# Norms and output products of a hybrid diffusion step: 1/rms in PSUM, squares added one tile late, biases on ScalarE, other banks and held weights

## The chip, the cores and the metric

The kernel runs on one core of a Trainium2 chip. Times are microseconds on the device, from the first to the last work of one execution. Lower is better. The core has five engines that work side by side, each in its own order: TensorE (PE, the matmuls; PEld is its loading of weights), VectorE (DVE), ScalarE (ACT), GpSimd (POOL) and SyncE (SP, which issues most of the DMAs). Matmuls write to PSUM, which the kernel divides into banks of 512 float32 columns; everything else lies in SBUF.

## The reference

One step of a small diffusion backbone with two layers. Text is 128 prompt tokens and 512 sample tokens with 1024 features. Layer 0 has an SSD mixer and a differential-attention mixer side by side, layer 1 an RG-LRU mixer; each is followed by a gated ConvFFN of width 2816. Each of the four sub-layers has this frame:

```python
def rmsnorm(x, g):
    xf = x.astype(jnp.float32)
    y = xf * lax.rsqrt(jnp.mean(xf * xf, axis=-1, keepdims=True) + EPS)
    return (y * g.astype(jnp.float32)).astype(x.dtype)

def modulate(h, shift, scale):
    return h * (1.0 + scale) + shift
```

The sub-layer's input is `modulate(rmsnorm(x), shift, scale)`. Its last step is an output product (1024 or 2816 features to 1024), multiplied by a gate and added to `x`. Shift, scale and gate come from a map of the conditioning vector, one set for prompt and one for samples.

## The kernel before

**Layout.** The residual `X` is one SBUF tile of 128 partitions x 8 feature tiles (kt) x 644 columns: 128 prompt columns, a gap of 4, 512 sample columns. A matrix product takes each operand as a high part and a rest (`hhi`, `hlo` of the text; `whi`, `wlo` or, for held weights, `hi`, `lo` of the weights), and makes three matmuls for each 128x128 tile of weights (L471, L472, L473). ACT casts a raw weight tile to its high part (L112, for held ones L126) and POOL subtracts for the rest (L117, L129) in pieces of 256 columns: four for a weight of 8 kt, two for one of 4 kt.

**Order of the work.** The program is written out by hand as one order. `after(n, f)` puts a step `f` n ticks later, a tick being the matmuls of one kt; so the steps of a norm are strewn between matmuls. Each engine runs what it got in that order, and waits by semaphores.

**Weights.** Raw tiles come through a ring of 3; split ones have 3 slots too. A weight marked "held" goes to a pool of its own (`W.over`), which is open only during the output product, so that both column parts can use it.

**Output products (`out_parts`).** The columns are cut into two parts (`hf` 0: the prompt and some of the samples; 1: the rest). In layer 0 and at the LRU's output these are 388 and 256 columns, at FFN 0's last down-projection 260 and 384. For each part come 8 output tiles in pairs, with PSUM from `bank(n)` (two `g` banks, in layer 0) or `wide_banks(n)`. Then `evac` empties each: DVE adds the gated product to `X` (`add_part`, L317), ACT squares it (L537, `sqt`), DVE adds the square to `sq` (L538).

**Norm (`norm_part`).** When all 8 tiles of a part are there: PE sums the squares over the partitions (L555), DVE makes mean plus epsilon (L557), POOL takes the power -1/2 (L559, `rstd`), PE spreads 1/rms over the partitions (L566) and ACT copies it from PSUM to SBUF, over `sq` (L570). Then `gen(kt)` for each kt: DVE multiplies 1/rms, scale and `X` (L317, `full` or `sqt` from `sq`), ACT adds the shift (L601). For an even kt the sum goes to `hhi` at once and DVE makes `hlo` with the shift (two L317). For an odd kt ACT adds it in place, casts to `hhi` (L604), and POOL makes `hlo` (L69). `low(kt-1)`, the making of `hlo`, stands behind the products of kt. Part 0's norm runs while PE does part 1 of the output product; PE may begin the next stage only after its last step (`k.fresh[0]`).

**The FFN's first products** use sums and differences of the normed tiles (`sums`, L1499 to L1503), which need the shift in `full` for all kt: for the even ones L1499 adds it. `part` makes `t24h` and `t24l` of one of them. The weights are summed likewise (`wsum`), and their parts are `shi` and `slo`.

**Map steps.** The map of the conditioning vector is done in small steps (`M.step`, `mt<-mraw`) between other products; `small()` gives them a PSUM bank, "m" or "o", which the norm uses too.

## Time and profile before

| | |
|---|---|
| median of 3 runs | 2109.64 us (2108.07 to 2111.09) |
| the profiled execution | 2112.0 us |
| its span in the trace | 2109.2 us |
| mean granted clock of TensorE | 0.956 of full speed |
| busy: PE | 1890.8 us (90%) |
| busy: DVE | 1431.1 us (68%) |
| busy: ACT | 963.7 us (46%) |
| busy: POOL | 1188.8 us (56%) |

The span reaches from the first to the last instruction; the execution's own time is 2.8 us longer. The busy share says how much of the span an engine worked. [...]

### The profile page before, as it was taken

To read this page: it belongs to the slowest core of one execution; us is meant where nothing else is said; L and a number is where in the kernel's file an instruction comes from. 1 tells how busy PE (TensorE), PEld (TensorE's weight loads), DVE (VectorE), ACT (ScalarE), POOL (GpSimd) and SP (SyncE) were. 2 spreads that over 40 slices of the span, in tenths; PEclk is the share of its full clock that TensorE was granted. 3 is DMA by queue.
4 is the path that set the end of the run, shared out by engine and by line. 5 is a ranking of instruction groups with operands and counts; after the bars stand their busy time and mean duration, and the time that the engine had idled before them with its cause. 6 is when DMAs were issued, how large, how long until landed. Compare 5 with 4: busy or idle time off the path is not lost. (4 is left out here: it accounts for less than half of the span.)

```text
span 2109.2 us, 33582 instructions
## 1 busy us (share of the span) xinstructions
PE 1890.8 (90%) x12601; PEld 1728.1 (82%) x12601; DVE 1431.1 (68%) x2454; ACT 963.7 (46%) x1670; POOL 1188.8 (56%) x1536
## 2 busy tenths in 40 slices
PE   6878889999999988999999997988778899999997
PEld 4767768888888877898889997877678799999986
DVE  3477756656664346687778787667857777877874
ACT  3454444455454334343344445577734444444444
POOL 3235454233344544477657785578855577776772
PEclk9889999999999998999999999999989899999998
DMA  9555432121113432435642222211111122222221
GB/s 257 171 164 164 151 108 66 49 55 48 38 49 122 127 123 71 125 121 163 187 141 63 72 87 75 60 46 46 40 50 41 44 76 81 85 87 70 62 78 63
DMA packets 255577, 196.59 MB, mean 93 GB/s; under 512 B 13837, under 2 KB 233816, under 8 KB 255288
## 3 DMA queue, kind: packets, MB, share of 16 engines
q1 hardware_dynamic: 252664, 184.59, 29.1%
q0 software_dynamic: 2528, 7.13, 1.4%
q8 instruction: 99, 1.62, 0.3%
q10 hardware_dynamic: 224, 2.73, 0.3%
q14 instruction: 62, 0.51, 0.1%
HBM read 187.50 MB, written 6.92 MB: 92 GB/s over the span
## 5 line engine op out<-in xcount | busy, mean ns | idle before, releaser
L117 POOL TENSOR_TENSOR wlo<-wraw,whi 128x256 fp32r<-128x256 f32 (+1 forms) x845 | 714.7, 874 | 554.7 <-ACT whi L112 488.2
L471 PE MATMUL wide<-hhi,whi 128*128 128x322 f32 (+4 forms) x1072 | 360.2, 336 | 49.9 <-DVE X L317 22.9
L472 PE MATMUL wide<-hlo,whi 128*128 128x322 f32 (+4 forms) x1072 | 346.1, 323 | 7.7 <-DVE hlo L512 7.5
L473 PE MATMUL wide<-hhi,wlo 128*128 128x322 f32 (+4 forms) x1072 | 342.7, 320 | 0.0
L112 ACT CAST whi<-wraw 128x1024 fp32r<-128x1024 f32 (+2 forms) x263 | 220.1, 838 | 146.3 <-PE wide L473 73.9
L471 PEld LDWEIGHTS wide<-hhi,whi 128*128 128x128 f32 x1072 | 213.1, 199 | 69.0 <-issue 23.0
L471 PE MATMUL gh<-hhi,whi 128*128 128x322 f32 (+3 forms) x704 | 236.5, 336 | 9.3 <-ACT zt L1161 8.7
L472 PEld LDWEIGHTS wide<-hlo,whi 128*128 128x128 f32 x1072 | 212.3, 198 | 13.0 <-DVE hlo L512 9.0
L472 PE MATMUL gh<-hlo,whi 128*128 128x322 f32 (+3 forms) x704 | 220.9, 314 | 1.3 <-DVE hlo L512 1.0
L473 PE MATMUL gh<-hhi,wlo 128*128 128x322 f32 (+3 forms) x704 | 220.2, 313 | 0.0
L473 PEld LDWEIGHTS wide<-hhi,wlo 128*128 128x128 f32 x1072 | 212.7, 198 | 0.0
L471 PE MATMUL wide<-hidh,whi 128*128 128x322 f32 (+4 forms) x624 | 200.5, 321 | 2.2 <-DVE ft L1585 2.2
L472 PE MATMUL wide<-hidl,whi 128*128 128x322 f32 (+4 forms) x624 | 196.0, 314 | 1.6 <-DVE hidl L512 1.6
L473 PE MATMUL wide<-hidh,wlo 128*128 128x322 f32 (+4 forms) x624 | 196.0, 314 | 0.0
L317 DVE SCALAR_TENSOR_TENSOR ft<-ft,PC 128x643 f32<-128x643 f32 x160 | 168.1, 1072 | 37.5 <-ACT ft L1527 35.5
L471 PEld LDWEIGHTS gh<-hhi,whi 128*128 128x128 f32 (+1 forms) x704 | 133.9, 190 | 34.8 <-issue 21.3
L1527 ACT ACTIVATE ft<-ft,PC 128x644 f32<-128x644 f32 x80 | 74.0, 927 | 144.6 <-DVE ft L1592 133.7
L317 DVE SCALAR_TENSOR_TENSOR X<-wide,modc,X 128x128 f32<-128x128 f32 (+3 forms) x264 | 123.5, 511 | 22.7 <-PE wide L473 22.7
L472 PEld LDWEIGHTS gh<-hlo,whi 128*128 128x128 f32 (+1 forms) x704 | 133.6, 190 | 2.4 <-DVE hlo L512 1.2
L473 PEld LDWEIGHTS gh<-hhi,wlo 128*128 128x128 f32 (+1 forms) x704 | 133.3, 189 | 0.6
L471 PEld LDWEIGHTS wide<-hidh,whi 128*128 128x128 f32 x624 | 119.4, 191 | 15.9 <-issue 7.0
L112 ACT CAST shi<-wsum 128x512 fp32r<-128x512 f32 x120 | 72.7, 617 | 122.2 <-DVE wsum L141 110.8
(381 smaller groups left out, 4579.5 us busy)
## 6 DMA issues: line engine op xcount, KB each, us to landing
wraw<-in_ffn_w_up_dram SPq DMA_DIRECT2D x88, 512.0 KB
mraw<-in_w_mod_dram SPq DMA_DIRECT2D x80, 512.0 KB
wraw<-in_ssd_attn_w_in_dram SPq DMA_DIRECT2D x42, 512.0 KB
wraw<-in_ffn_w_down_dram SPq DMA_DIRECT2D x96, 192.0 KB
E<-ad SPq DMA_DIRECT2D x16, 640.0 KB
mraw<-in_w_mod_dram SPq DMA_DIRECT2D x32, 256.0 KB
wraw<-in_ssd_attn_w_out_dram SPq DMA_DIRECT2D x16, 512.0 KB
wraw<-in_lru_w_in_dram SPq DMA_DIRECT2D x16, 512.0 KB
```

Of the source, the lines that this page charges most:

```text
L112: self.nc.scalar.copy(hi, src)
L117: low.tensor_sub(lo[:, q], src[:, q], hi[:, q].bitcast(F32))
L317: nc.vector.scalar_tensor_tensor(out, in0, scalar, in1, op0=op0, op1=op1, **kw)
L471: nc.tensor.matmul(ps[:whi.shape[-1], p0:p0 + c1 - c0], whi, xhi[:, c0:c1], start=start, stop=False)
L472: nc.tensor.matmul(ps[:whi.shape[-1], p0:p0 + c1 - c0], whi, xlo[:, c0:c1], start=False, stop=False)
L473: nc.tensor.matmul(ps[:whi.shape[-1], p0:p0 + c1 - c0], wlo, xhi[:, c0:c1], start=False, stop=stop)
L1527: after(at, lambda: nc.scalar.activation(out, u, AF.Identity, scale=par(cw, 2 * NF + t), bias=par(cb, t)))
```

## The change

1. `rstd_rows` leaves 1/rms in PSUM (bank "o"); the norm's products read it there, and ACT's copies L570 go, but for the one place where attention's norm uses it.
2. While that bank is in use, map steps take bank "m" alone (`k.spread`).
3. The square of an output tile is added to `sq` when the next tile has been emptied (`add_square`), the last one when the sum is needed.
4. In norms whose tiles are kept for the FFN (`keep`), ACT adds the shift of even kt in place and casts, as for odd kt; DVE makes `hlo` of a whole part with one subtraction. The additions L1499 in `sums` go, and L1501 moves from POOL to DVE.
5. In layer 0's output product two pairs of output tiles in three take a wide PSUM tile.
6. Instead of 3 everywhere, the number of output weights that are not held is 2 in layer 0, none at FFN 0's last down-projection, and 3 in the other two. And the look-ahead for weights no longer stops at the output product's last weight (`base + 7`).

```diff
-N_STD = 3
+N_STD = (2, 0, 3, 3)
...
         if n == 0:
+            add_square()
             nc.scalar.activation(sq, X[:, n, c0:c1], AF.Square)
         else:
             t = k.tmp.tile([128, NT], F32, name="sqt", tag=k.sq_tag, bufs=k.n_sqt)[:, c0:c1]
             nc.scalar.activation(t, X[:, n, c0:c1], AF.Square)
+            add_square()
+            k.square = sq, t
+
+    k.square = None
+
+    def add_square():
+
+        if k.square:
+            (sq, t), k.square = k.square, None
             nc.vector.tensor_add(sq, sq, t)
...
     def small():
-        return mtile("m" if k.narrow else None)
+        return mtile("m" if k.narrow or k.spread else None)
...
-    def rstd_rows(r, hf):
-
-        m = mtile()
+    def rstd_rows(r, hf, tag):
+
+        m = mtile(tag)
         for i in range(len(k.cut.chunks[hf])):
             nc.tensor.matmul(m[:, 128 * i:128 * i + 128], r[:, i:i + 1].to_broadcast([128, 128]), ident,
                              start=True, stop=True)
-        at = 0
-        for _, c0, c1 in k.cut.segs[hf]:
-            nc.scalar.copy(k.sq[:, c0:c1], m[:, at:at + c1 - c0])
-            at += c1 - c0
+        return m
...
-            if kt % 2:
+            if kt % 2 or keep:
                 c = slice(*k.cut.parts[hf])
-                pieces(nc.gpsimd, "tensor_sub", lo[:, c], t[:, c], h[:, c].bitcast(F32))
+                if kt % 2:
+                    pieces(nc.gpsimd, "tensor_sub", lo[:, c], t[:, c], h[:, c].bitcast(F32))
+                else:
+                    nc.vector.tensor_sub(lo[:, c], t[:, c], h[:, c].bitcast(F32))
                 return
...
-                    fma(t[:, c0:c1], k.sq[:, c0:c1], A, X[:, kt, c0:c1], op0=OP.mult, op1=OP.mult)
-                    nc.scalar.activation((t if kt % 2 else hhi[kt])[:, c0:c1], t[:, c0:c1], AF.Identity, bias=B)
-                if kt % 2:
+                    fma(t[:, c0:c1], box.m[:, at:at + c1 - c0], A, X[:, kt, c0:c1], op0=OP.mult, op1=OP.mult)
+                    nc.scalar.activation((t if whole else hhi[kt])[:, c0:c1], t[:, c0:c1], AF.Identity, bias=B)
+                    at += c1 - c0
+                if whole:
                     c = slice(*k.cut.parts[hf])
                     nc.scalar.copy(hhi[kt][:, c], t[:, c])
...
-                            W.upto(min(base + i + AHEAD, base + 7))
+                            W.upto(base + i + AHEAD)
...
+        turn = []
+
         def bank(n):
+
+            if n == 2:
+                turn.append(0)
+            if n == 2 and len(turn) % 3:
+                return wide_banks(2)
             return [k.psum.tile([128, 512], F32, name="gh", tag="g", bufs=2) for _ in range(n)]
...
                 x, y = full[kt], full[kt + 4]
-                if kt % 2 == 0:
-                    for i, t in ((kt, x), (kt + 4, y)):
-                        for s, cols in STREAMS:
-                            nc.vector.tensor_scalar(t[:, cols], t[:, cols], modc[l][:, s, 24 + i:25 + i], None, op0=OP.add)
                 nc.vector.tensor_sub(x[:, L], x[:, R], x[:, L])
-                nc.gpsimd.tensor_sub(x[:, R], y[:, R], x[:, R])
+                nc.vector.tensor_sub(x[:, R], y[:, R], x[:, R])
                 nc.vector.tensor_sub(y[:, R], y[:, R], x[:, L])
```

What this does to the order of the instructions is seen at three places. In the rows that follow, L317 is the helper for a multiply and add, and the lines of the changed kernel are some ten higher than those of before.

DVE, in part 1 of layer 0's output product, just ahead of the emptying of the third pair of output tiles (the first `X<-` in each). Before:

```order
L597 MEMSET full 128x4
L317 SCALAR_TENSOR_TENSOR full<-sq,acol_115,X 128x128
L317 SCALAR_TENSOR_TENSOR full<-sq,acol_115,X 128x256
L317 SCALAR_TENSOR_TENSOR hlo_88<-full,modc_112,hhi_80 128x128
L317 SCALAR_TENSOR_TENSOR hlo_88<-full,modc_112,hhi_80 128x256
L317 SCALAR_TENSOR_TENSOR X<-gh,modc_112,X 128x256
L538 TENSOR_TENSOR sq<-sq,sqt 128x256
```

The same place after the change:

```order
L607 MEMSET full 128x4
L317 SCALAR_TENSOR_TENSOR full<-mt,acol_115,X 128x128
L317 SCALAR_TENSOR_TENSOR full<-mt,acol_115,X 128x256
L597 TENSOR_TENSOR hlo_88<-full,hhi_80 128x388
L317 SCALAR_TENSOR_TENSOR X<-wide,modc_112,X 128x256
L548 TENSOR_TENSOR sq<-sq,sqt 128x256
```

The products read 1/rms from `mt` (PSUM), `hlo` is one operation, and the third pair stands in a wide tile; the norm's steps are still ahead of the emptying. The fourth pair takes `gh`, as the first did.

ACT, at the start of FFN 0's last down-projection, where the last hidden tile (`hidh`, the second of the two in the rows of before) is still being made: L1527 (L1550 after) are its convolutions, L1543 (L1566) its gate. Before:

```order
L112 CAST whi<-wraw 128x512
L508 CAST hidh<-ft 128x644
L112 CAST whi<-wraw 128x512
L1527 ACTIVATE ft<-ft,PC 128x644
L126 CAST hi_12883<-wraw 128x512
L1527 ACTIVATE ft<-ft,PC 128x644
L126 CAST hi_12902<-wraw 128x512
L126 CAST hi_12921<-wraw 128x512
L1543 ACTIVATE ft<-ft 128x644
L126 CAST hi_12939<-wraw 128x512
L508 CAST hidh<-ft 128x644
L126 CAST hi_12960<-wraw 128x512
```

After:

```order
L508 CAST hidh<-ft 128x644
L1550 ACTIVATE ft<-ft,PC 128x644
L126 CAST hi_12851<-wraw 128x512
L126 CAST hi_12858<-wraw 128x512
L126 CAST hi_12865<-wraw 128x512
L126 CAST hi_12872<-wraw 128x512
L1550 ACTIVATE ft<-ft,PC 128x644
L126 CAST hi_12891<-wraw 128x512
L126 CAST hi_12910<-wraw 128x512
L1566 ACTIVATE ft<-ft 128x644
L126 CAST hi_12928<-wraw 128x512
L508 CAST hidh<-ft 128x644
```

The casts `whi` of this product's first weights are gone; four held casts stand between the two convolutions, where one stood.

POOL, from the rests of the held weights of that product (`lo`) to the norm of part 0 behind it (`rstd` and the rests of odd kt, `hlo`); `wlo` are weights of the next stage. Before:

```order
L129 TENSOR_TENSOR lo_12940<-wraw,hi_12939 128x256 x2
L129 TENSOR_TENSOR lo_12961<-wraw,hi_12960 128x256 x2
L559 TENSOR_TENSOR rstd<-msq,expo 128x2
L69 TENSOR_TENSOR hlo_83<-sqt,hhi_75 128x130 x2
L69 TENSOR_TENSOR hlo_85<-sqt,hhi_77 128x130 x2
L117 TENSOR_TENSOR wlo<-wraw,whi 128x256 x12
L69 TENSOR_TENSOR hlo_87<-sqt,hhi_79 128x130 x2
```

After:

```order
L129 TENSOR_TENSOR lo_12929<-wraw,hi_12928 128x256 x2
L129 TENSOR_TENSOR lo_12950<-wraw,hi_12949 128x256 x2
L117 TENSOR_TENSOR wlo<-wraw,whi 128x256 x12
L570 TENSOR_TENSOR rstd<-msq,expo 128x2
L69 TENSOR_TENSOR hlo_83<-sqt,hhi_75 128x130 x2
L69 TENSOR_TENSOR hlo_85<-sqt,hhi_77 128x130 x2
L69 TENSOR_TENSOR hlo_87<-sqt,hhi_79 128x130 x2
```

The twelve `wlo` have moved from between the `hlo` to ahead of `rstd`; and eight `lo` of two pieces each stand ahead of them, where there were five.

## Rows read from the trace of the kernel before

**Rows 1.** Page, part 1: busy us, share of the span, instructions of each engine.

```profile
PE 1890.8 (90%) x12601; PEld 1728.1 (82%) x12601; DVE 1431.1 (68%) x2454; ACT 963.7 (46%) x1670; POOL 1188.8 (56%) x1536
```

**Rows 2.** Waits of PE, 730 to 800: who ended them, total us, times, longest.

```profile
PE gh L471 <- DVE X L317: 9.2, 5, 5.6
```

**Rows 3.** Timeline of PE: start, us, instruction, and the idle time before it.

```profile
744.37 0.42 PE L471 MATMUL gh<-hhi,hi 128*128 128x388 f32 x1 [1.29 <-DVE X L317]
```

**Rows 4.** Timeline of DVE, 760 to 800 us.

```profile
775.34 0.48 DVE L317 SCALAR_TENSOR_TENSOR full<-sq,acol,X 128x256 f32<-128x256 f32 x1
...
783.36 0.81 DVE L317 SCALAR_TENSOR_TENSOR full<-sq,acol,X 128x128 f32<-128x128 f32 x1
...
784.09 0.95 DVE L317 SCALAR_TENSOR_TENSOR full<-sq,acol,X 128x256 f32<-128x256 f32 x1
784.97 1.71 DVE L317 SCALAR_TENSOR_TENSOR hlo<-full,modc,hhi 128x128 fp32r<-128x128 f32 x2
...
791.38 0.47 DVE L317 SCALAR_TENSOR_TENSOR X<-gh,modc,X 128x256 f32<-128x256 f32 x1
```

**Rows 5.** Windows: busy time of each engine, granted clock (PEclk), DMA share, GB/s.

```profile
789.40:796.20 6.80, 4.30 (x20) 4.30 (x21) 3.70 (x7) 1.89 (x5) 4.38 (x7) 0.50 0.52 153
1315.00:1328.60 13.60, 7.84 (x36) 7.87 (x37) 5.42 (x11) 2.98 (x6) 7.02 (x13) 0.50 0.35 96
1598.40:1605.10 6.70, 5.06 (x17) 5.09 (x18) 1.11 (x4) 0.42 (x1) 0.70 (x1) 0.50 0.01 1
```

**Rows 6.** Waits of PE, 833 to 863 us.

```profile
PE wide L471 <- ACT shi L112: 3.8, 1, 3.8
```

**Rows 7.** Timeline of DVE, 825 to 837 us, in the sums.

```profile
825.83 1.26 DVE L1499 TENSOR_SCALAR full<-full,modc 128x128 f32<-128x128 f32 x4
...
828.50 1.01 DVE L1502 TENSOR_TENSOR full<-full 128x322 f32<-128x322 f32 x1 [0.99 <-POOL full L1501]
...
836.60 0.49 DVE L1502 TENSOR_TENSOR full<-full 128x322 f32<-128x322 f32 x1 [1.04 <-POOL full L1501]
```

**Rows 8.** Timeline of PE, first matmul of the LRU's input product.

```profile
1320.76 0.56 PE L471 MATMUL wide<-hhi,whi 128*128 128x260 f32 x1 [7.90 <-DVE X L317]
```

**Rows 9.** Timeline of ACT, 1271 to 1330 us.

```profile
1274.11 0.93 ACT L1527 ACTIVATE ft<-ft,PC 128x644 f32<-128x644 f32 x1 [2.53 <-DVE ft L1592]
```

**Rows 10.** Timeline of POOL, 1271 to 1330 us.

```profile
1275.66 10.41 POOL L129 TENSOR_TENSOR lo<-wraw,hi 128x256 fp32r<-128x256 f32 x10
1297.29 0.70 POOL L559 TENSOR_TENSOR rstd<-msq,expo 128x2 f32<-128x2 f32 x1 [11.22 <-DVE msq L557]
...
1308.43 9.26 POOL L117 TENSOR_TENSOR wlo<-wraw,whi 128x256 fp32r<-128x256 f32 x12 [2.89 <-issue]
1317.64 2.02 POOL L69 TENSOR_TENSOR hlo<-sqt,hhi 128x130 fp32r<-128x130 f32 x4
```

**Rows 11.** Timeline of DVE, 1271 to 1330 us.

```profile
1287.18 0.43 DVE L538 TENSOR_TENSOR sq<-sq,sqt 128x260 f32<-128x260 f32 x1 [0.48 <-ACT sqt L537]
...
1300.53 0.88 DVE L317 SCALAR_TENSOR_TENSOR sqt<-sq,acol,X 128x128 f32<-128x128 f32 x3
...
1310.21 2.32 DVE L317 SCALAR_TENSOR_TENSOR sqt<-sq,acol,X 128x128 f32<-128x128 f32 x3
...
1314.65 0.60 DVE L317 SCALAR_TENSOR_TENSOR X<-wide,modc,X 128x384 f32<-128x384 f32 x1
```

**Rows 12.** Waits of PE, 1593 to 1662 us.

```profile
PE wide L471 <- DVE lt L1856: 6.8, 1, 6.8
```

**Rows 13.** Timeline of DVE, 1593 to 1604 us.

```profile
1596.55 0.43 DVE L538 TENSOR_TENSOR sq<-sq,sqt 128x256 f32<-128x256 f32 x1 [0.48 <-ACT sqt L537]
```

**Rows 14.** Timeline of ACT, 784 to 800 us: bias on 128 and 256 columns, cast.

```profile
784.20 0.40 ACT L601 ACTIVATE full<-full,modc 128x128 f32<-128x128 f32 x1 [0.36 <-DVE full L317]
785.08 0.51 ACT L601 ACTIVATE full<-full,modc 128x256 f32<-128x256 f32 x1 [0.48 <-DVE full L317]
785.62 0.52 ACT L604 CAST hhi<-full 128x388 fp32r<-128x388 f32 x1
```

More of the change, by code (lines that the diff above doesn't have):

```diff
@@ L364, in add_w, with held @@
         items.append((ap[r0:r0 + 128 * kt, c0:c0 + w], kt, w, kind))
-    def held(n, n_std=3):
+    def held(n, n_std):
         return "held" if n >= n_std else None
@@ L394, in tile_hybrid_step @@
         for n in range(8):
-            add_w(w_out, 1024 * half, 8, 128 * n, kind=held(n, N_STD) if half else None)
+            add_w(w_out, 1024 * half, 8, 128 * n, kind=held(n, N_STD[0]) if half else None)
     def early(c):
@@ L414, in downs @@
             for n in range(8):
-                add_w(dn, 128 * starts[c], FF_CHUNKS[c], 128 * n, kind=held(n, N_STD) if last else None)
+                add_w(dn, 128 * starts[c], FF_CHUNKS[c], 128 * n, kind=held(n, N_STD[1 + 2 * l]) if last else None)
         for c, n in enumerate(FF_CHUNKS):
@@ L430, in tile_hybrid_step @@
     for n in range(8):
-        add_w(lw_out, 0, 8, 128 * n, kind=held(n))
+        add_w(lw_out, 0, 8, 128 * n, kind=held(n, N_STD[2]))
     ffn_items(1)
@@ L546, in small @@
     def small():
-        return mtile("m" if k.narrow else None)
+        return mtile("m" if k.narrow or k.spread else None)
     def rstd_cols(chunks):
-        m = mtile()
+        add_square()
+        m = mtile("m")
         n = len(chunks)
@@ L597, in gen @@
                     nc.vector.memset(t[:, NP:S0], 0.0)
+                whole, at = kt % 2 or keep, 0
                 for s, c0, c1 in segs:
                     A, B = acol[l][which][:, s, kt:kt + 1], modc[l][:, s, 24 * which + kt:24 * which + kt + 1]
[L600 to L602 removed]
+                    fma(t[:, c0:c1], box.m[:, at:at + c1 - c0], A, X[:, kt, c0:c1], op0=OP.mult, op1=OP.mult)
+                    nc.scalar.activation((t if whole else hhi[kt])[:, c0:c1], t[:, c0:c1], AF.Identity, bias=B)
+                    at += c1 - c0
+                if whole:
                     c = slice(*k.cut.parts[hf])
@@ L607, in gen @@
             k.fresh[hf] = kt == KD
+            k.spread = k.spread and kt < KD
             if kt == KD and then:
@@ L611, in norm_part, with rows @@
         after(at[0], cols)
-        after(at[0] + at[1], lambda: rstd_rows(box.r, hf))
+        def rows():
+            k.spread = True
+            box.m = rstd_rows(box.r, hf, "o")
+        after(at[0] + at[1], rows)
         for kt in range(KD + 1):
             after(at[0] + at[1] + at[2] + at[3] * kt, lambda kt=kt: gen(kt))
-    k.fresh = [True, True]
+    k.fresh, k.spread = [True, True], False
     k.cut = Cut(CUTS[0])
@@ L643, in gemm_parts, with out_parts @@
                     W.ahead()
-    def out_parts(xs, evac, then, banks, first, ready, n_std=N_STD):
+    def out_parts(xs, evac, then, banks, first, ready, n_std):
         ws, base = [], W.next
@@ L671, in out_parts @@
                     if j == len(late) - 1:
-                        W.upto(min(base + batch[-1][-1] + AHEAD, base + 7))
+                        W.upto(base + batch[-1][-1] + AHEAD)
                         break
@@ L1372, in rows @@
                 for hf in range(2):
-                    rstd_rows(rs[hf], hf)
+                    m, at = rstd_rows(rs[hf], hf, "m"), 0
+                    for _, c0, c1 in k.cut.segs[hf]:
+                        nc.scalar.copy(k.sq[:, c0:c1], m[:, at:at + c1 - c0])
+                        at += c1 - c0
                 for t in range(KD):
@@ L1440, in attention @@
         hctx = ExitStack()
-        out_parts(H, evac, then, bank, [[0], [1]], [ready])
+        out_parts(H, evac, then, bank, [[0], [1]], [ready], N_STD[0])
         W.over = None
@@ L1636, in then @@
                         until(lambda: k.fresh[0])
-                out_parts(xs, evac, then, wide_banks, [[0, 1], [2, 3], [4, 5]], [ready])
+                out_parts(xs, evac, then, wide_banks, [[0, 1], [2, 3], [4, 5]], [ready], N_STD[1 + 2 * l])
                 W.over = None
@@ L1849, in then @@
                     until(lambda: k.fresh[0])
-            out_parts(H, evac, then, wide_banks, [[0, 1], [2]], [lambda: until(lambda: len(k.scanned) == 8 and k.n_given == 14), ready], 3)
+            out_parts(H, evac, then, wide_banks, [[0, 1], [2]], [lambda: until(lambda: len(k.scanned) == 8 and k.n_given == 14), ready], N_STD[2])
             W.over = None
```

1 line of the change is left out of this document (removed).

## The prediction

> **What bounds the kernel now.** I read the page first: TensorE (PE) is busy 1890.8 us, nine tenths of the span [rows 1]. So work on another engine is worth only the PE idle time that it ends, plus what PE loses because its clock falls behind such a pause. Then I asked for PE's waits in the four stretches in which an output product ends, a norm is made and the next stage begins: 730 to 800 us (layer 0's output product) [rows 2], 833 to 863 us (the sums of FFN 0's first products) [rows 6], 1271 to 1330 us (FFN 0's last down-projection and the norm of layer 1) [rows 8], and 1593 to 1662 us (the LRU's output product and FFN 1's sums) [rows 12]. In three of the four, what ends the largest wait is DVE with an `X` (L317), an accumulator waiting to be emptied, or something that stands right behind such ones. Last I read the timelines of DVE, ACT and POOL in those stretches, to see what stands ahead of that instruction, and windows for the clock.
>
> **Stage A, layer 0's output product and FFN 0.** Two causes are added up in [rows 2]: 9.2 us in 5 waits.
>
> *More banks.* Before, each pair of output tiles takes both `g` banks, so the next pair starts only after DVE has emptied one. In column part 0 that costs PE 1.29 us [rows 3], twice in this form; with a smaller one it is 3.0 us. With two pairs in three in the wide banks, the next pair has a bank that was emptied long ago. I take 2.9; the bounds are 0 (if the wide bank is emptied as late) and 3.0.
>
> In column part 1 the longest wait, 5.6 us [rows 2], has another head: DVE came to the evacuation only at 791.38 us [rows 4], because the order shown above puts tiles of the norm ahead of it. The last pair now goes to the `g` banks, which pair 0 left long before; what stands ahead of the evacuation on DVE no longer holds PE. The 5.6 us go, and about 0.6 of small ones. [...] Sum for this place 8.3. It is worth this only if the norm of part 0 is also finished by then, since PE may not go on to FFN 0 before: that takes DVE's norm steps being shorter.
>
> *1/rms read from PSUM.* The trace has no DVE operation with 1/rms in PSUM. Nearest rows: `X<-gh` has one operand in PSUM and takes 0.47 us for 256 columns while POOL runs; `full<-sq`, both in SBUF, takes 0.95 for 256 while POOL runs and 0.48 alone [rows 4]. The bounds for the new form are thus 0.47 and 0.95; I take 0.47, since its operands are of the kinds of `X<-gh`. Four tiles of 0.81 + 0.95 [rows 4] then become 0.34 + 0.47 (by the same ratio), 3.8 us less on DVE. The two `hlo` of an even tile (1.71 together [rows 4]) become one subtraction. That one has two SBUF inputs; its bounds are 0.49 and 1.01, from the 322-column rows [rows 7], and I take 0.9. So DVE has about 5 us less ahead of the last norm step, and the norm ends in time.
> [...]
>
> *ACT's added work.* An even tile now has two biases and a cast, 0.40 + 0.51 + 0.52 = 1.43 us for 388 columns [rows 14], as an odd tile has already. For eight tiles that is 11.4 us against 9.4. Cover: part 1 of the output product, 192 matmuls of 256 columns. The copies L570 leave ACT. In part 1's own norm, which nothing covers, ACT's work per tile is about as long as DVE's was; I count it at nothing, bounds -1 and +1.
>
> *Sums.* Two of the four sums lose four L1499 (1.26 us), and each loses a wait of 1.0 us for POOL, for which a DVE operation of 0.49 comes [rows 7]. What stands behind the last of them is `t24h`, then the cast `shi`, for which PE waited 3.8 us [rows 6]. Not all eight L1499 and four waits lie on that chain, since DVE does other work between the sums; what moves `shi` is one 1.26 and two times 0.5, 2.3. I take 2.4, bounds 1 and 4. Behind it POOL's `slo` may be late next.
>
> Stage A: -2.9 - 8.3 - 2.4 = **-13.6** (bounds -5 and -17).
>
> **Stage B, FFN 0's last down-projection, the norm, the LRU.** Here a part of the change costs time. All eight weights are now held, and a held weight's cast is issued only within this output product. Before, PE began with weights cast earlier. Now all four first casts stand behind the convolution of 1274.11 us on ACT [rows 9], and the fourth, whose raw tile has no place until POOL has done the first, stands ahead of the gate's convolution. I estimate that `hid[21]` is ready 4 us later, and hence the first evacuation too.
> What comes back: in each tile's cycle of evacuation, ACT square and DVE add, DVE waits 0.48 us for the square [rows 11]. With the add one tile late that goes; eight tiles give 3.8 us. So the sum of squares is ready about when it was.
> Then POOL: `rstd` came at 1297.29, after ten `lo` pieces of 1.04 us from 1275.66 on [rows 10]. Sixteen end at about 1292, and the twelve `wlo` (9.26 us [rows 10]), which came after `rstd`, now come ahead of it: about 1302. That is 5 us later. But before, the `wlo` ran against the norm: three `sqt<-sq` took 2.32 us against 0.88 elsewhere [rows 11], and POOL's last `hlo` ended only at 1319.66 [rows 10]. In the same stretch the evacuation from PSUM still took 0.60 us [rows 11]. Now eight tiles at about 1 us of ACT each end near 1312, PE's part 1, which ended at 1312.9 before (1320.76 less the wait, [rows 8]), near 1315, the last evacuation near 1317. PE went on at 1320.76, after 7.9 us of waiting [rows 8]; I take 1318, -2.7. The lower clock behind that wait lasted 13.6 us, with PE busy 7.84 of it [rows 5], a loss of 3.9; a third of it back, -1.3. Stage B: **-4** (bounds -8 and +8; the upper one if `rstd` comes as late as 1311).
> [...]
>
> **Stage C, the LRU's output product and FFN 1.** PE waited 6.8 us for `lt` [rows 12], which stands behind four evacuations on DVE, each with a wait of 0.48 us for its square [rows 13]: 1.9 us less. Ahead of them stand norm steps as in stage A, some 3 us shorter. I take -4.8 (bounds -2 and -6). Of 6.7 us at 0.50 with PE busy 5.06 [rows 5], 2.5 come back. The sums are those of FFN 0: -2.4. Stage C: **-9.7** (bounds -4 and -12).
>
> The rest: map steps have almost none in these stretches, so leaving bank "o" alone costs nothing; if some did come, one would wait for the DVE add of the one before. The last FFN's evacuations save little, since PE waits there for another step. 0.
>
> **Sum.** -13.6 - 4 - 9.7 = -27.3. The profiled execution took 2112.0 us, so 2084.7; it lies 2.4 us above the median of the runs, 2109.64, from which the same sum gives 2082.3. I forecast 2083 (own range 2074 to 2093).
>
> **Rivals.**
> *The norm, not the bank, is late (0.17).* PE gets its banks, runs to the end of the product and waits there for the norm of part 0, whose pace ACT now sets. For: ACT has 2 us more in that norm, plus casts. Against: 5 us less on DVE, which was the slower. Half of 8.3 and of 4.8 + 2.5 would be lost: about 2091; with the sums' gain gone into `slo` too, 2096.
> *Reads from PSUM are dear (0.04).* If the new form takes the upper bound, 0.95 in place of 0.47, DVE's norm steps stay as long as beside POOL, and the 3.8 us that were to make each norm end in time are missing in stages A and C: 2091. Against: 0.47 and 0.60 for `X` [rows 4, 11]. [...]
> *The held weights turn stage B into a loss (0.12).* `rstd` waits on POOL behind `wlo`, which waits for raw tiles that can be fetched only when the last `lo` are done. Stage B at +8 in place of -4: 2095. It decides from a `rstd` later than about 1306 us.
> *Slower (0.10).* DVE works in order, and the subtraction of an even tile now waits for two biases and a cast on ACT, where it waited for one bias at a time. If that wait is not covered, a tile goes in series: 0.82 + 1.43 + 0.9 and hops, 3.3 us against about 2 in [rows 4], 9 us more a norm, with the evacuations behind it on DVE. Stages A and C would lose their gain at the banks and at `lt` and 9 us each besides, stage B its 4: about 2120. It decides when ACT needs over 2 us for a tile with its square and the weights' casts between. Against it: the subtraction stands behind the next tile's products on DVE, so a tile's time is there to cover it.
>
> **Chances.** Forecast 0.57, the rivals 0.17 + 0.04 + 0.12 + 0.10. The first three rivals end below 2100, the last above. About 0.2% (4 us) is what a measurement of this kernel can tell. Faster by more than that 0.82, within it 0.07 (the tails of the rivals), slower 0.11. The range takes the forecast's lower end, a little widened, 2072, and reaches to 2102 over the milder rivals.
>
> **What would show it.** In the profile after: no wait of PE for `X` of over 1 us in the output product of layer 0, and no stretch at half clock at its end; `full<-mt` at 0.34 and 0.47 us also beside POOL; DVE's waits for `sqt` gone; in stage B a later first evacuation, a later `rstd`, and a wait of PE before the LRU of about 5 us; in stage C a wait of about 2 us for `lt`. I am wrong if PE waits for the norm at the end of these products as long as it waited for the banks, or if stage B loses more than 8 us.

## The result and the profile after

The changed kernel takes 2080.66 us (median of 4 runs, 2078.34 to 2080.81), the kernel before beside it 2110.27; the ratio is 0.9857, with a 95% interval of 0.9844 to 0.987. Measured once more (`after_again`) it came to 0.9854 (0.9837 to 0.9871). The forecast was 2083, 2072 to 2102.

The page of the changed kernel, part 1, answers to [rows 1]:

```profile
PE 1880.9 (90%) x12601; PEld 1719.6 (83%) x12601; DVE 1415.1 (68%) x2438; ACT 964.7 (46%) x1677; POOL 1184.0 (57%) x1528
```

The matmuls are the same; PE's 10 us less of busy time go with a mean granted clock of 0.962 for 0.956 (the clock that TensorE was granted, 1 being its full speed). The rest of the gain lies in the waits. PE's waits in layer 0's output product, 720 to 800 us, against [rows 2]:

```profile
PE mt L332 <- DMA mraw<-in_w_mod_dram: 2.7, 1, 2.7
...
PE wide L471 <- DVE X L317: 0.7, 1, 0.7
```

Of the 9.2 us for `X` in the product nothing is left; the 0.7 belongs to the start of FFN 0 and stood in the kernel before too, at 800.43 us. But a wait stands there that the kernel before did not have: 2.7 us for the weights of a map step (`mraw`), in part 0. DVE's timeline in part 1 of the same product, against [rows 4]:

```profile
782.60 0.56 DVE L597 TENSOR_TENSOR hlo<-full,hhi 128x388 fp32r<-128x388 f32 x1 [2.54 <-ACT hhi L616]
...
783.35 0.47 DVE L317 SCALAR_TENSOR_TENSOR full<-mt,acol,X 128x256 f32<-128x256 f32 x1
783.74 0.47 DVE L317 SCALAR_TENSOR_TENSOR X<-wide,modc,X 128x256 f32<-128x256 f32 x1
...
789.91 0.48 DVE L317 SCALAR_TENSOR_TENSOR X<-wide,modc,X 128x256 f32<-128x256 f32 x1
```

`full<-mt` takes 0.47 us with POOL at work, and DVE reaches the third pair of output tiles, which stands behind norm steps, at 789.91 us (791.38 before). The first row shows the new wait of the change: `hlo` stands 2.54 us for ACT's cast, between weight casts. PE has no wait for `X` in this product, so it is covered. Over the whole program (groups by line and form: count, busy us, mean ns), before and then after:

```profile
L317 DVE SCALAR_TENSOR_TENSOR full<-sq,acol,X 128x256 f32<-128x256 f32 x32 | 19.1, 618 | 5.8 <-ACT sq L570 5.8
```

```profile
L317 DVE SCALAR_TENSOR_TENSOR full<-mt,acol,X 128x256 f32<-128x256 f32 x32 | 14.5, 474 | 3.9 <-PE mt L577 3.9
```

FFN 0's last down-projection and the LRU's start: PE's waits of 1255 to 1315 us, then ACT, DVE and POOL there, against [rows 8 to 11]:

```profile
PE wide L471 <- ACT hi L126: 3.9, 1, 3.9
...
PE wide L471 <- DVE X L317: 0.8, 1, 0.8
```

```profile
1266.62 1.64 ACT L126 CAST hi<-wraw 128x512 fp32r<-128x512 f32 x3
1271.71 0.62 ACT L126 CAST hi<-wraw 128x512 fp32r<-128x512 f32 x1 [3.44 <-DMA wraw<-in_ffn_w_down_dram]
```

```profile
1284.83 0.44 DVE L548 TENSOR_TENSOR sq<-sq,sqt 128x260 f32<-128x260 f32 x1
1285.19 0.59 DVE L317 SCALAR_TENSOR_TENSOR X<-wide,modc,X 128x128 f32<-128x128 f32 x2
```

```profile
1288.16 5.91 POOL L117 TENSOR_TENSOR wlo<-wraw,whi 128x256 fp32r<-128x256 f32 x8 [1.40 <-ACT whi L112]
1294.02 0.70 POOL L570 TENSOR_TENSOR rstd<-msq,expo 128x2 f32<-128x2 f32 x1
```

PE now waits 3.9 us at the front for the held casts; the fourth cast waits 3.44 us for its raw tile, with the second convolution behind it. DVE's square adds hardly wait any more. `rstd` stands behind the `wlo`. At the end the wait before the LRU is 0.8 us in place of 7.9. In the LRU's output product, 1570 to 1640 us, against [rows 12]:

```profile
PE wide L471 <- ACT shi L112: 4.2, 1, 4.2
...
PE wide L471 <- DVE lt L1879: 1.4, 1, 1.4
```

And the granted clock behind these three places (windows; the third figure from the right is PEclk), against [rows 5]:

```profile
788.40:795.00 6.60, 5.93 (x50) 5.76 (x49) 4.30 (x11) 3.57 (x9) 2.21 (x4) 1.00 0.01 4
...
1309.00:1323.00 14.00, 12.98 (x98) 12.58 (x99) 8.87 (x18) 7.95 (x15) 6.56 (x13) 1.00 0.13 29
1578.00:1585.00 7.00, 5.59 (x36) 5.43 (x34) 2.98 (x8) 1.44 (x4) 3.72 (x6) 1.00 0.29 85
```

Where 0.50 stood there is 1.00.

**By stage.** PE runs the same 12601 matmuls in the same order in all kernels here, so the start of the n-th marks the same place of the program. The stages are cut at matmuls 4560, 5700 (A); 8060, 8670 (B); 9560, 10100 (C); 12380 and the last (D), which in the kernel before start at 726.9, 916.6; 1263.8, 1391.0; 1586.6, 1692.4; 2056.1 us. The table gives each kernel's profiled execution minus that of before, in us; "rest" is all that lies outside these stages, from the first matmul on.

| kernel | A | B | C | D | rest |
|---|---|---|---|---|---|
| forecast | -13.6 | -4 | -9.7 | 0 | 0 |
| after | -10.5 | -7.1 | -10.5 | -5.1 | +3.0 |
| after_again | -10.9 | -8.6 | -10.5 | -3.8 | +4.8 |
| u_banks | -9.8 | -7.8 | -10.5 | -6.6 | +2.8 |
| u_square | -9.2 | -0.2 | -6.6 | -1.3 | +5.8 |
| u_bias | -10.6 | -6.9 | -7.5 | -6.7 | +3.7 |
| u_psum | -13.0 | -6.0 | -10.3 | -5.1 | +7.3 |
| p_banks | -2.8 | -1.4 | 0.0 | -1.3 | +6.0 |
| p_square | -5.8 | -6.0 | -6.7 | -5.1 | +5.0 |
| p_psum | -4.1 | -2.4 | -3.4 | 0.0 | -1.3 |
| h0 | -13.7 | -7.6 | -10.4 | -3.8 | +1.6 |
| h1 | -12.4 | -7.4 | -10.4 | -5.2 | +7.0 |
| h31 | -13.1 | -7.2 | -10.4 | -5.3 | +1.8 |
| h32 | -14.6 | -5.6 | -10.0 | -5.3 | +1.2 |

The rest moves by over 8 us between kernels that are nearly the same there, so stages tell more than whole times. A stage's number is good to about 2 us: `after`, `after_again` and `h1` run the same in stage A and lie 1.9 apart. In B the boundary at matmul 8670 flatters five kernels (after_again, u_square, u_psum, p_banks, p_psum) by 1.6 to 1.8 us, which come back in the rest: counted up to the start of C, `after` stands at -7.1 and `after_again` at -6.9.

Some of the readings below need pieces of two stages: A from its start to matmul 4900 (part 0 and the start of part 1), 4900 to 5000 (the long wait of part 1 and the clock behind it) and 5200 to 5300 (the sums); B up to matmul 8310, the first of the LRU, and from there on (the share of B's boundary is in this last column). Again in us, minus the kernel before:

| kernel | A to 4900 | 4900 to 5000 | 5200 to 5300 | B to the LRU | B from the LRU |
|---|---|---|---|---|---|
| forecast | -2.9 | -8.3 | -2.4 | -2.7 | -1.3 |
| after | +0.5 | -7.8 | -2.8 | -3.3 | -3.8 |
| after_again | -1.4 | -7.8 | -2.6 | -3.2 | -5.4 |
| u_banks | +0.9 | -7.3 | -2.6 | -3.9 | -3.8 |
| u_square | -1.6 | -5.0 | -2.6 | +3.6 | -3.8 |
| u_bias | -1.3 | -7.8 | -0.3 | -3.1 | -3.8 |
| p_banks | -3.1 | -1.2 | +0.3 | 0.0 | -1.4 |
| p_square | -0.8 | -4.3 | +0.3 | -7.6 | +1.6 |
| h0 | -4.2 | -7.6 | -2.6 | -3.8 | -3.8 |
| h1 | -2.0 | -7.8 | -3.2 | -10.6 | +3.3 |
| h31 | -3.7 | -7.6 | -2.6 | -6.7 | -0.5 |
| h32 | -3.8 | -7.6 | -2.6 | -5.5 | -0.1 |

### The profile page after: what moved, and what is told of

The parts are those of the page before. It is cut to its first block, busy times and chain, and to the rows that moved or that the text cites. A ratio compares the mean times of both kernels' runs of the same rounds, so it can differ in the third digit from the quotient of the medians.

```text
span 2078.7 us, 33613 instructions
## 1 busy us (share of the span) xinstructions
PE 1880.9 (90%) x12601; PEld 1719.6 (83%) x12601; DVE 1415.1 (68%) x2438; ACT 964.7 (46%) x1677; POOL 1184.0 (57%) x1528
## 5 line engine op out<-in xcount | busy, mean ns | idle before, releaser
L112 ACT CAST whi<-wraw 128x1024 fp32r<-128x1024 f32 (+1 forms) x259 | 217.4, 840 | 146.2 <-PE wide L473 71.1
L471 PE MATMUL gh<-hhi,whi 128*128 128x322 f32 (+3 forms) x688 | 232.1, 337 | 8.7 <-ACT zt L1178 8.7
L472 PE MATMUL gh<-hlo,whi 128*128 128x322 f32 (+3 forms) x688 | 216.4, 315 | 1.3 <-DVE hlo L512 1.0
L473 PE MATMUL gh<-hhi,wlo 128*128 128x322 f32 (+3 forms) x688 | 215.9, 314 | 0.0
L317 DVE SCALAR_TENSOR_TENSOR ft<-ft,PC 128x643 f32<-128x643 f32 x160 | 167.3, 1067 | 42.6 <-ACT ft L1550 40.6
L471 PE MATMUL wide<-hidh,whi 128*128 128x322 f32 (+2 forms) x600 | 191.3, 319 | 1.1 <-DVE ft L1608 1.1
L472 PE MATMUL wide<-hidl,whi 128*128 128x322 f32 (+2 forms) x600 | 187.0, 312 | 0.8 <-DVE hidl L512 0.8
L473 PE MATMUL wide<-hidh,wlo 128*128 128x322 f32 (+2 forms) x600 | 187.0, 312 | 0.0
L317 DVE SCALAR_TENSOR_TENSOR X<-wide,modc,X 128x128 f32<-128x128 f32 (+3 forms) x276 | 128.0, 507 | 33.8 <-PE wide L473 33.8
L1550 ACT ACTIVATE ft<-ft,PC 128x644 f32<-128x644 f32 x80 | 73.9, 927 | 145.4 <-DVE ft L1615 135.3
L471 PEld LDWEIGHTS wide<-hidh,whi 128*128 128x128 f32 x600 | 113.5, 189 | 14.5 <-issue 7.0
```

The lines of the kernel that those rows point to most:

```text
L112: self.nc.scalar.copy(hi, src)
L317: nc.vector.scalar_tensor_tensor(out, in0, scalar, in1, op0=op0, op1=op1, **kw)
L471: nc.tensor.matmul(ps[:whi.shape[-1], p0:p0 + c1 - c0], whi, xhi[:, c0:c1], start=start, stop=False)
L472: nc.tensor.matmul(ps[:whi.shape[-1], p0:p0 + c1 - c0], whi, xlo[:, c0:c1], start=False, stop=False)
L473: nc.tensor.matmul(ps[:whi.shape[-1], p0:p0 + c1 - c0], wlo, xhi[:, c0:c1], start=False, stop=stop)
L1550: after(at, lambda: nc.scalar.activation(out, u, AF.Identity, scale=par(cw, 2 * NF + t), bias=par(cb, t)))
```

## The experiments

**Theory** (from the prediction): each part gives what its waits cost, and the banks give most in layer 0. **Rival**: the parts all empty the same queue, DVE's, so that most are worth little beside the others, and one of them carries the gain. The first four take one part out of the changed kernel. No run takes out the longer look-ahead for weights or gives bank "o" back to map steps, so what these two are worth is not shown.

**u_banks.** The `g` banks for every pair.

```diff
-            if n == 2 and len(turn) % 3:
-                return wide_banks(2)
```

> The changed kernel, but layer 0's output product takes the two g banks for every pair again. My theory, by the sum of the prediction: the waits for X come back, 1.3 us each in part 0, and in part 1 one of several us with a stretch at half clock behind it; 6 to 9 us longer than the changed kernel, about 2088. Rival: DVE's norm steps are so much shorter now that the evacuation is no longer late in part 1, and only part 0's 2 to 3 us come back, about 2083.

Measured: 2082.47 us, ratio 0.986 (0.9842 to 0.9879); the changed kernel has 0.9857. PE's waits of 725 to 800 us:

```profile
PE gh L471 <- DVE X L317: 4.2, 4, 1.4
```

The 5.6 us of part 1 are 1.4 without the banks, and the piece 4900 to 5000, where in the kernel before a granted clock of 0.50 followed that wait, is 7.3 us shorter. Part 0's waits come back, but the wait for `mraw` falls from 2.7 to 0.2 us. Stage A loses 0.7 to 1.1 us, of which the piece with the long wait 0.5. The rival holds: with the other parts in place the banks are worth about 1 us, which is within the scatter.

**u_square.** Each square is added at once.

```diff
-            k.square = sq, t
+            nc.vector.tensor_add(sq, sq, t)
```

> The changed kernel, but each square is added at once again. My theory: DVE waits about 0.48 us for the square at each of the 7 tiles of 8 parts; on the path of PE are those of FFN 0's last down-projection (3.5 us), of the LRU's output product (about 1.5) and, as the trace of after shows against the prediction, of the last down-projection with the half clock behind it (up to 4.6): 7 to 10 us longer, about 2089. Rival: the other parts have made DVE early enough, so that the waits are covered: under 3 us.

Measured: 2097.67 us, ratio 0.9929 (0.9911 to 0.9946), 17 us longer than the changed kernel: more than either theory. Stage B loses nearly all of its gain (the LRU starts 6.9 us later than in the changed kernel), C and D lose 3.9 and 2.5 to 3.8 us, A 1.3 to 1.7. PE's waits in stage B:

```profile
PE mt L566 <- DVE sq L540: 3.9, 1, 3.9
PE wide L471 <- DVE X L317: 3.4, 1, 3.4
```

The wait before the LRU is back at 3.4 us, although all else that was to shorten it is in place.

**u_bias.** Shifts of even tiles as before.

```diff
-            if kt % 2 or keep:
+            if kt % 2:
...
-                whole, at = kt % 2 or keep, 0
+                whole, at = kt % 2, 0
...
+                if kt % 2 == 0:
+                    for i, t in ((kt, x), (kt + 4, y)):
+                        for s, cols in STREAMS:
+                            nc.vector.tensor_scalar(t[:, cols], t[:, cols], modc[l][:, s, 24 + i:25 + i], None, op0=OP.add)
...
-                nc.vector.tensor_sub(x[:, R], y[:, R], x[:, R])
+                nc.gpsimd.tensor_sub(x[:, R], y[:, R], x[:, R])
```

> The changed kernel, but the shifts of even feature tiles are added as before (L1499 in the sums, two operations on DVE for the rest, one operation of each sum on POOL). My theory: the two waits of PE at the sums for the cast shi are longer by 2.4 us each, about 5 us in all, 2086. Rival: in FFN 1 the wait for shi was as long after the change as before, so something else sets it, and only FFN 0's 2.4 us come back: 2083.

Measured: 2088.67 us, ratio 0.9885 (0.9866 to 0.9904), 6 to 8 us longer than the changed kernel; the profiled execution, 2082.84 us, was one of its shortest. In its trace stage C loses 3.0 us. Stage A as a whole shows nothing, but only because part 0 came out 1.8 us shorter than in the changed kernel: there the granted clock was 0.89 in the 15 us around the wait for `mraw`, here 1.00. In the piece with the sums 2.5 us are lost. PE's wait there, in the changed kernel and in this one:

```profile
PE wide L471 <- ACT shi L112: 1.3, 1, 1.3
```

```profile
PE wide L471 <- ACT shi L112: 3.6, 1, 3.6
```

So the theory holds, with 2.5 and 3.0 us for its 2.4 twice, and the rival, that only FFN 0's part comes back, is refuted by FFN 1. Of the 6 to 8 us by whole time the 1 to 2 that are left are not explained.

**u_psum.** ACT copies 1/rms to SBUF.

```diff
-            box.m = rstd_rows(box.r, hf, "o")
+            m, at = rstd_rows(box.r, hf, "o"), 0
+            for _, c0, c1 in segs:
+                nc.scalar.copy(k.sq[:, c0:c1], m[:, at:at + c1 - c0])
+                at += c1 - c0
...
-                    fma(t[:, c0:c1], box.m[:, at:at + c1 - c0], A, X[:, kt, c0:c1], op0=OP.mult, op1=OP.mult)
+                    fma(t[:, c0:c1], k.sq[:, c0:c1], A, X[:, kt, c0:c1], op0=OP.mult, op1=OP.mult)
```

> The changed kernel, but ACT copies 1/rms from PSUM to SBUF again and the norm's products read it there. My theory: the products take longer beside POOL (0.62 us against 0.47 on average for 256 columns), and each of the norms of part 1, which nothing covers, starts about 0.9 us later: 4 to 7 us longer, about 2086. [...]

Measured: 2082.9 us, ratio 0.9855 (0.9838 to 0.9873), the same as the changed kernel. Its products do take longer (groups by form):

```profile
L317 DVE SCALAR_TENSOR_TENSOR full<-sq,acol,X 128x256 f32<-128x256 f32 x32 | 17.7, 573 | 4.8 <-ACT sq L629 4.8
```

0.573 us on average from SBUF, against 0.474 from PSUM in the changed kernel (alone one took 0.48 us from SBUF, [rows 4]). So in this program the products that read PSUM were not the dearer ones, which speaks against the prediction's rival "reads from PSUM are dear"; but the whole time is the same, so the time that they save is covered now, and with it my 4 to 7 us.

The next two put one part alone into the kernel before.

**p_banks.** The lines that u_banks takes out, in the kernel before.

> The kernel before with one part of the change: layer 0's output product takes the wide banks for two pairs in three. By the sum of the prediction: up to 11 us less (the 2.9 of part 0, 5.6 and a little more of part 1, 2.1 of the clock), about 2099, with no wait for X over 1 us there. Rival: without the shorter norm steps PE runs ahead, waits at the end of part 1 for the norm or the last evacuation, and part 0's gain is taken by the wait for a map step's weights that the changed kernel shows at 749: 2 to 5 us less, about 2107.

Measured: 2106.55 us, ratio 0.9977 (0.9965 to 0.9989). PE at the start of FFN 0:

```profile
798.37 0.66 PE L471 MATMUL wide<-hhi,whi 128*128 128x388 f32 x1 [5.37 <-DVE X L317]
```

The wait of 5.6 us has become one of 5.4 at the end of the product: PE has its banks early and stands until DVE has worked off the same queue. What it waits for is the last emptying, not the norm's end, which comes 2.2 us earlier with POOL's last `hlo`:

```profile
793.54 2.63 POOL L69 TENSOR_TENSOR hlo<-full,hhi 128x194 fp32r<-128x194 f32 x4
```

```profile
797.75 0.48 DVE L317 SCALAR_TENSOR_TENSOR X<-gh,modc,X 128x256 f32<-128x256 f32 x1
```

Stage A gains 2.8 us. The rival is right in its amount and its place; it left open whether the norm or the last emptying is late, and it is the emptying.

**p_square.** The delayed add alone.

```diff
+            add_square()
+            k.square = sq, t
+
+    k.square = None
+
+    def add_square():
+
+        if k.square:
+            (sq, t), k.square = k.square, None
             nc.vector.tensor_add(sq, sq, t)
...
     def rstd_cols(chunks):
 
+        add_square()
```

> The kernel before with one part of the change: each square is added one tile late. If its worth doesn't hang on the other parts, what taking it out of the changed kernel cost (some 16 us) comes off here: about 2094. Rival: it is worth that only where the other parts have emptied DVE's queue; beside the longer norm steps it takes 0.48 us a tile from each of the four products, of which 3.5 us at FFN 0's last down-projection, 2 at the LRU's output and 3 to 4 at the end are on PE's path: about 2101.

Measured: 2093.97 us, ratio 0.9925 (0.9908 to 0.9942): 18.7 us less than the kernel before by the medians, 16 by the ratio, more than half of what the whole change gives. The theory holds: it doesn't hang on the other parts. Taken out, it costs 17 by the medians, 15 by the ratios.

**p_psum.** 1/rms in PSUM alone; the core of the diff is the reverse of that of u_psum. Map steps also leave its bank alone here, as they do in u_psum.

> The kernel before with one part of the change: 1/rms stays in PSUM and the norm's products read it there; map steps leave its bank alone. My theory after the runs without the banks: DVE's queue ahead of the evacuation, not the bank, is what the 5.6 us of the kernel before come from; with the products at 0.47 us beside POOL the wait in part 1 shrinks to 1 to 3 us with no change of banks, and each norm of part 1 starts 0.9 us earlier: 5 to 9 us less than the kernel before, 0.9965. Rival: the squares' waits alone keep DVE late, and the part is worth under 3 us.

Measured: 2103.98 us, ratio 0.9966 (0.9953 to 0.9979), 7.6 us less. PE's waits of 725 to 800 us:

```profile
PE gh L471 <- DVE X L317: 6.4, 5, 3.0
```

The longest is 3.0 in place of 5.6, with the banks of before: DVE's queue made that wait, as the theory had it. So u_psum and this one together: the part is worth 7 to 8 us alone, and nothing beside the delayed add and the rest.

The last ones are on the held weights.

**h0 and h1.** The number of weights not held:

```diff
-N_STD = (2, 0, 3, 3)
+N_STD = (3, 0, 3, 3)   # h0
+N_STD = (2, 3, 3, 3)   # h1
```

> The changed kernel, but layer 0's output product holds its weights from the fourth on, as before, in place of the third. My theory on the 2.7 us that PE waits for a map step's weights in part 0: one weight more is held there, so that its output weights are fetched earlier and the map's later; with the old number the DMAs stand in another order, and the wait goes or shrinks under 1 us: 1 to 3 us less than the changed kernel, about 2078.5. Rival: the wait comes from PE being early (the banks no longer hold it) while the DMA queues set the pace: the wait stays over 2 us, and the time is the same.

> The changed kernel, but FFN 0's last down-projection holds its weights from the fourth on, as before, in place of all. By the prediction holding all costs 3 us at its start and 4 us until the last hidden tile, and brings the weights' rests out of the norm's way: without it the first evacuation comes 4 us earlier, rstd too, but twelve pieces of the next weights run beside the norm again. With 1/rms in PSUM these no longer slow the norm: 3 to 5 us less than the changed kernel, about 2077. Rival: POOL's last rests of the norm stand behind those twelve pieces again and the LRU starts no earlier: the same or up to 3 us more.

Measured: h0 2080.96 us, ratio 0.9856 (0.9838 to 0.9875); h1 2079.19 us, ratio 0.9851 (0.9833 to 0.987). In whole time neither stands out from the changed kernel. In the trace of h0, PE's waits of 725 to 800 us have this in place of 2.7:

```profile
PE mt L332 <- DMA mraw<-in_w_mod_dram: 0.2, 1, 0.2
```

and stage A is about 3 us shorter, at -13.7. That is shown for the place: up to matmul 4900 the three kernels with the old number (h0, h31, h32) have -3.7 to -4.2, those with the new one and the wide banks -2.0 to +0.5. For the whole time only h31 speaks. In h1 the wait of 3.9 us at the front of stage B is gone (1.1 us for another step remain), and at the end stands:

```profile
PE mt L566 <- DVE sq L548: 3.9, 1, 3.9
PE wide L471 <- DVE X L317: 2.9, 1, 2.9
```

The stage is as long as before this edit. The granted clock in windows of 21 us that begin 4 us before the LRU's start, first of h1, then of the changed kernel:

```profile
1300.00:1321.00 21.00, 14.20 (x90) 13.70 (x89) 11.72 (x23) 8.12 (x17) 13.13 (x23) 0.76 0.36 94
```

```profile
1305.00:1326.00 21.00, 19.60 (x136) 18.89 (x135) 14.55 (x36) 12.09 (x24) 8.16 (x15) 1.00 0.09 20
```

The theory's first half came: the LRU starts 7.3 us earlier than in the changed kernel (-10.6 against -3.3). Then all of it is lost, in the wait of 3.9 us, which stands just behind the LRU's first matmuls, and at the lower clock. The rival is right on the amount and on the cause. The last squares on ACT wait for tiles that POOL's `hlo` give free, and these stand behind the twelve pieces:

```profile
1306.92 0.53 ACT L538 ACTIVATE sqt<-X 128x384 f32<-128x384 f32 x1 [4.42 <-POOL hlo L69]
```

It is wrong in one point, that the LRU starts no earlier.

**after_again, h31, h32.** The changed kernel and two more numbers, together on one chip.

```diff
-N_STD = (2, 0, 3, 3)
+N_STD = (3, 1, 3, 3)   # h31
+N_STD = (3, 2, 3, 3)   # h32
```

> The changed kernel once more, on the same chip and beside the same runs of the kernel before as the next three, since the scatter between chips is as large as what tells them apart. About 0.986 of the kernel before.

> The changed kernel, with 3 weights not held in layer 0's output product (as before; the map step's wait of 2.7 us was gone in that trace) and 1 not held at FFN 0's last down-projection. My theory on the latter: what delayed the last hidden tile by 4 us is the fourth held cast, which waits on ACT for a raw tile; with the first weight cast ahead of time a place in the ring is free earlier, the cast doesn't wait, and most pieces of the next weights still come ahead of rstd: PE reaches the LRU some 3 us earlier, layer 0 gives 3 more, 4 to 6 us less than the changed kernel, 0.983. Rival: as with 3 not held there, what is gained at the front is lost at the end to the evacuations: only layer 0's part, 0.985, or nothing.

> As the kernel before this one in the list, but 2 weights not held at FFN 0's last down-projection. By my theory the front is as early or half a us earlier, but eight pieces of the next weights in place of four stand between rstd and POOL's rests of the norm: the LRU starts 0 to 2 us later than with 1 not held, 0.984. Rival: no difference between the two.

Measured: after_again 2080.41 us, 0.9854 (0.9837 to 0.9871); h31 2075.0 us, 0.9831 (0.9814 to 0.9848); h32 2078.89 us, 0.9847 (0.9831 to 0.9863). h31 is the shortest of all and lies 5.4 us below the changed kernel by its median; the two intervals overlap a little. Its theory on stage B came half true: the LRU starts some 3.4 us earlier than in the changed kernel, but the stage, with -7.2, is no shorter. PE's waits there:

```profile
PE wide L471 <- DVE X L317: 1.9, 1, 1.9
PE wide L471 <- ACT hi L126: 1.9, 1, 1.9
```

The front has 1.9 for 3.9 us, the LRU's start 1.9 for 0.8, and the granted clock around it is

```profile
1299.00:1320.00 21.00, 19.05 (x118) 18.65 (x117) 13.18 (x34) 10.36 (x20) 7.78 (x15) 0.84 0.09 20
```

So what is gained at the front is lost behind the LRU's start (-0.5 against -3.8), as the rival had it. What its trace gains on the changed kernel lies in stage A, 2.6 us, as in h0; the rest of the 5.4 is not explained. In h32 the LRU starts 1.2 us later than in h31, within the 0 to 2 that were expected.

## Why the prediction was right, and where not

The time was forecast within 2.4 us, but of the four stages' terms three were off, and so was the nothing for the rest. That they cancelled is luck.

**Stage A, -13.6; measured -10.5 and -10.9.** The term for part 0, 2.9, failed (+0.5 and -1.4): it named as bounds 0 and 3.0 only what the banks do, and left out what PE meets when it is no longer held. It met the map's weights, 2.7 and 2.4 us. With the old number of held weights this wait is 0.2 to 0.7 us and the stage measured -13.7, -13.1 and -14.6 (h0, h31, h32), the sum as forecast; so the one weight more that is held is the main cause. The order of the DMAs fits: SyncE issues a map step's weights 1.8 us after PE's last map step in the changed kernel (745.99 against 744.18), and 0.3 us ahead of it in h0 (742.23 against 742.52). It is not the only cause: in p_banks, which has the old number too, the wait was 1.3 us. The 8.3 for part 1 came (-7.8), but I gave them to the wrong part. The sentence "what stands ahead of the evacuation on DVE no longer holds PE" does not hold for the banks by themselves: in p_banks 5.4 us of wait move to the end. And u_banks has 7.3 of the 7.8 us without them, so DVE's shorter queue alone did it. These shorter steps stand in the prediction only as a condition; they were the cause. The 2.1 us in the 8.3 are for the clock, my estimate: half of PE's 4.30 us at 0.50 in [rows 5]. No run shows this share by itself; what the traces show in its place are matmuls of 128x256 that start every 0.21 us at 0.50 (before, 793 to 796 us) and every 0.12 us at 1.00 (before, 797 us; after, 789 to 791 us).

**1/rms in PSUM.** 0.47 us was right (mean 0.474, where the copy gives 0.573); the 0.34 for 128 columns came too (mean 0.341), though the ratio that the prediction names would give 0.40. Of the rivals, "reads from PSUM are dear" is refuted: its 0.95 did not come. Copied to SBUF first (u_psum), the whole time was the same (0.9855 against 0.9857). What no step of the prediction saw: beside the other parts this one is worth nothing, where alone it is worth 7.6 us.

**Stage B, -4; measured -7.1 and -8.6 (-6.9 up to the start of C).** The mechanism was as forecast. The changed kernel enters this stage 8.0 us earlier (matmul 8060 at 1255.8 against 1263.8 us); put back by that, its first evacuation comes at 1281.97 + 8.0 = 1290.0 us (4.4 later than before, 4 were estimated), `rstd` at 1302.0 (about 1302), and the LRU starts at 1309.43 + 8.0 = 1317.4 (I took 1318). The mis-sized term is the clock: not a third but all of the 3.9 us came back (3.8 from the LRU's start on, with a granted clock of 1.00 there); the wait that was left was 0.8 us and not 5. The 5 among the prediction's signs did not fit its own times, 1318 less 1315. That holding all weights costs something at the front is shown; that it costs on the whole is not (h1, h31: -7.4 and -7.2).

**Stage C, -9.7; measured -10.5 twice.** Right: `lt` 1.4 us (about 2 forecast), a granted clock of 1.00 behind it. In the sums the size was right too (-2.7 for -2.4; u_bias loses 3.0), but not the place: `shi` went only from 4.6 to 4.2 us. What ended was another wait, for a step of FFN 1's convolution on DVE, here before and in u_bias; in the changed kernel it is gone:

```profile
PE wide L471 <- DVE ft L317: 2.2, 1, 2.2
```

```profile
PE wide L471 <- DVE ft L317: 1.7, 1, 1.7
```

In FFN 0 `shi` was the place, from 3.8 to 1.3.

**Stage D, 0; measured -5.1 and -3.8.** The step "the last FFN's evacuations save little, since PE waits there for another step" failed. That step, ACT's `xg`, stands on ACT behind a square, which waits for DVE's `X`, which stood behind an add waiting for the square of the tile before. ACT and DVE before, and DVE after, where the add finds its square done:

```profile
2068.78 0.53 ACT L537 ACTIVATE sqt<-X 128x388 f32<-128x388 f32 x1 [0.77 <-DVE X L317]
```

```profile
2069.34 0.57 DVE L538 TENSOR_TENSOR sq<-sq,sqt 128x388 f32<-128x388 f32 x1 [0.60 <-ACT sqt L537]
```

```profile
2043.24 0.55 DVE L548 TENSOR_TENSOR sq<-sq,sqt 128x388 f32<-128x388 f32 x1
```

PE's waits in the last 50 us and the window over them, before and after:

```profile
PE mt L1875 <- ACT xg L1899: 7.4, 8, 1.6
```

```profile
2060.00:2109.00 49.00, 34.07 (x203) 30.66 (x201) 20.60 (x46) 24.84 (x54) 7.58 (x9) 0.84 0.16 61
```

```profile
PE mt L1898 <- ACT xg L1922: 5.4, 6, 1.6
```

```profile
2030.00:2079.00 49.00, 35.36 (x226) 31.79 (x224) 23.97 (x49) 26.15 (x57) 12.18 (x14) 0.92 0.19 70
```

2 us of waits are gone. As an estimate, with only the 0.50 of [rows 5] and the 1.00 of the windows after: a mean clock of 0.84 over 49 us is 16 us at 0.50, and 0.92 is 8 us; with PE busy some 0.7 of the time (34.07 and 35.36 of 49 us) and about half as fast at 0.50 (0.21 against 0.12 us between matmuls, stage A), the 8 us less give back about 3. In u_square the stage is only 1.3 us shorter than before, and p_square alone has -5.1, so both come from the delayed add.

**The squares** are the term most too small. I counted 3.8 us in stage B and 1.9 in C; put in or taken out they are worth 15 to 19, and alone (p_square) they give 5.8, 6.0, 6.7 and 5.1 in the four stages. The 0.48 us a tile is right. But behind DVE's waits come more than themselves: in u_square, where they are back, PE waits 3.4 us for `X` before the LRU in place of 0.8, and the granted clock over the last 48 us is 0.88, in the changed kernel 0.92 over the last 49.

**The rest, 0; measured +3.0 and +4.8 (3.1 if B reaches to the start of C).** The prediction did not see that the delayed add also stands in another norm, that of the SSD mixer's output at 335 to 345 us. There it costs time. Only two tiles hold squares there, and an add that comes one tile later keeps its tile longer, so ACT's last square now waits for it, and PE for the sum. ACT after, then PE's waits of 325 to 350 us, before and after:

```profile
336.69 0.74 ACT L538 ACTIVATE sqt<-X 128x644 f32<-128x644 f32 x1 [2.59 <-DVE sq L548]
```

```profile
PE mt L555 <- DVE sq L538: 0.8, 1, 0.8
```

```profile
PE mt L566 <- DVE sq L548: 1.7, 1, 1.7
```

From matmul 2040 to 2100 nine of the ten kernels with the delayed add are 2.4 us longer than before, and p_square 3.8; u_square and p_psum are 0.0. Of the 2.4 us 0.9 are this wait; the rest goes with a granted clock of 0.84 in place of 1.00, here before and after:

```profile
335.00:345.00 10.00, 8.93 (x62) 8.32 (x62) 4.35 (x9) 3.64 (x8) 6.65 (x10) 1.00 0.21 59
```

```profile
334.00:345.00 11.00, 9.05 (x53) 8.68 (x52) 3.77 (x7) 2.69 (x5) 6.62 (x10) 0.84 0.21 54
```

In p_banks, which has the old add, 1.5 us were lost there too, so that share can come without the new one.

**The slower rival** (DVE in line behind ACT): the wait exists, 2.54 us at 782.60, and was covered, as the argument against it said.

## What to carry to other kernels

- Look for waits inside an engine's queue, and at what stands behind them. Here moving the consumer of another engine's result one step later (the square's add) was worth about half of the whole gain, alone as well as taken out, and more than any other part that was tested. In the norm that has only two tiles for the squares it cost 2.4 us; whether a third tile would save them was not tried.
- When several edits empty the same queue, don't add up their worth: price one by what is left of the wait after the others, and test it both ways, alone and taken out. Here the banks and 1/rms in PSUM gave about 5 and 7 us alone, and 1 and 0 taken out. More buffers in front of a late engine moved the wait (p_banks: 5.6 us became 5.4 at the end of the product); they did not end it.
- Ask what the released engine meets next. Here that was the weights of a map step, 2.7 us, which another part of the same change had moved back (with its old number 0.2 to 0.7).

## What the runs showed that I had not expected

Parts outside the stages differ by 8 us between executions (the table's last column, -1.3 to +7.3), about as much as single parts of the change are worth; without the 2.4 us of the delayed add it is still 7. Much of it arises in the first 90 us, after which the kernels lie from 4.1 us ahead of the kernel before to 1.9 behind it. PE waits there for the map's weights, of the kernel before and of p_psum, the one furthest ahead:

```profile
PE mt L332 <- DMA mraw<-in_w_mod_dram: 9.4, 5, 4.6
```

```profile
PE mt L332 <- DMA mraw<-in_w_mod_dram: 4.2, 3, 3.3
```

And short waits went with a lower clock: in stage B, a wait of 0.8 us left the granted clock at 1.00 around the LRU's start, while waits of 1.9 (h31) and of 2.9 and 3.9 us (h1) went with 0.84 and 0.76 in windows of 21 us; from the LRU's start on, stage B was 3.3 and 7.1 us longer there than in the changed kernel.
